# Output weights loaded during the projection's last phase, activation rows loaded far ahead, and another load table for phase 2's weights, in a hybrid decoder layer

## The chip, the cores and the metric

The kernel runs on one core of a Trainium2 chip. The metric is the time of one execution on the device in microseconds (us). The engines go by the profile's names: PE (matmul; PEld is its weight load), DVE (vector), ACT (scalar), POOL (GpSimd) and SP, which here only issues DMAs. Each engine takes its instructions in the order of its own list.

## The reference

One layer of a decoder is computed for 4096 prompt tokens and 64 sample tokens. All is fp32.

```python
h = rmsnorm(x, g_pre)                     # x: 4096 (and 64) x 1024
z = h @ w_in                              # 1024 x 2816, cut into ten column groups
out_a = silu(cg) * cb * conv3(cc * ch)    # gated short convolution
out_b = silu(ag) * window_attention(q, k, v, sinks)   # window of 128, 8 heads, 2 kv heads
out_c = silu(mg) * cross_attention(mq, mem_k, mem_v)  # 4 heads, 256 memory tokens
y = concat([out_a, out_b, out_c]) @ w_out # 1024 x 1024
x = x + rmsnorm(y, g_post)
```

Memory keys and values come from another normalised product (`w_mem_kv`). The last rows of the window's keys and values and of the convolution's input are outputs as well.

## The kernel before, in words

**Precision.** A matmul operand is split in two parts: hi, a cast to fp32r on ACT, and lo, the rest, a subtract on DVE. A product is three matmuls: hi by hi, lo by hi, hi by lo. `w_split` (L144) does so for a weight tile of 128x512: `S.copy` (L145) and `V.tensor_tensor` (L146).

**Input projection.** The 4160 tokens are 8 blocks of 520. The 22 column groups of 128 of `w_in` are taken as 11 pairs in three phases: phase 1 (index 0) has 4 pairs, phase 2 (index 1) 4 and phase 3 (index 2) 3. Within a phase each block is computed by seven block products in the manner of Strassen and Winograd (`PRODUCTS`): the weights A11, A12, A22 come from `w_in`, S1 to S4 are sums of them; the activations are B11 to B22 and their sums T1 to T4. In each step of a block one product is done for each pair (L305), and its result is added to z (`evict`, L312 on DVE, L314 on ACT). A step (phase, block, product) is the unit of all tables. The first two blocks of phase 1 are "plain": eight steps (block, step) each, since the sums of weights are made beside them. `plain_jobs` (L554) lists what ACT, DVE and POOL do after each plain step, `plain_loads` (L584) what SP loads. In phases 1 and 2 the order of each engine's list is that of the program. In phase 3 and in attention a scheduler sets it.

**Row statistics.** Each token needs 1/rms of its row. The rows (104 at a time) are loaded by `row_load` (L208) into `nat` tiles of a pool with two buffers; `row_step` squares and sums one (ACT L227), asks for the load two further on, and after five of them POOL computes r (L231, L232) and stores it to DRAM as `rowd` (L236). `row_queue` (L253) issues the waiting nat loads and the loads of `rb` (L206), r spread over all partitions. For the first blocks r goes to the token axis through a diagonal (`rows_diag`, DVE L243) and a product (`rows_product`, PE L249, ACT L251). After that, x is scaled ahead of the split (L271, L275) instead of z behind the product; this is the type change.

**Weights.** Split weights lie in two pools of slots of 4 KB per partition: `wa` (21 slots, pairs 0 to 2) and `wb` (7 slots, pair 3). Raw weights are loaded (`w_load` L152) into `temp` tiles, which the gates `th` (L365, L366), their stores to `md` and z's halves use too. The table `SWITCH` (L752) says in which steps phase 2's weights are loaded (`next_loads`, into `temp` tiles, or with `True` into the two nat buffers) and split (`next_fills`); `last` is block 7. POOL issues the stores of th to `md` until phase 2 begins, SP from then on.

**Attention.** `open_attention` (L828) closes the projection's pools and opens `fix` (constants, and `wo`, the split output weights), `mixp` (three buffers of `mix`, 1 MB each, L920), and `wor` (three raw buffers). 16 chunks of 256 tokens go through window units (L998 to L1031) and cross units (L958 to L973) of a pipe. In the first two chunks, each of 16 starts of the pipe also issues one load of half a row group of `w_out` (`wo_load`, L1047) and the split of the one before (`wo_split`, L1052 on ACT, L1053 on DVE). After them come the blocks of the output projection: `mix` is split to `mh` and `ml` (L1252, L1253), multiplied by `wo` (L1270), normalised and stored, with the units of later chunks in between.

Of the kernel before, what the change touches and what calls it, by code (L numbers as in the profile page):

```python
# [51 lines left out]
def hybrid_layer(ctx: ExitStack, tc: tile.TileContext, a: dict):  # L52
# [31 lines left out]

    pa = ExitStack()
    wa = pa.enter_context(tc.tile_pool(name="wa", bufs=3 * NP_))
# [57 lines left out]
    def w_split(w, raw):  # L144
        S.copy(w[:, 0], raw)  # L145
        V.tensor_tensor(w[:, 1], raw, f(w[:, 0]), op=ALU.subtract)  # L146
# [53 lines left out]
    nat, sq = {}, [0]  # L200
# [7 lines left out]
    def row_load(j):  # L208
        if j < 5 * NBLK:
            g = RG * j - NS  # L210
            t = nat[j] = natp.tile([P, D], F32, tag="nat", name=f"nat{j}")
            if g < 0:
                DMA.dma_start(t[:NS], a["x_s"])
                DMA.dma_start(t[NS:RG], a["x_p"][: RG - NS, :])
            else:
                DMA.dma_start(t[:RG], a["x_p"][g : g + RG, :])

    def row_step():
# [9 lines left out]
        row_loads.append(j + 2)  # L228
# [251 lines left out]
    def next_block(ph, b, p):  # L480
# [11 lines left out]
        if ph == 0:  # L492
            jobs.append(row_queue)
            if 1 <= p < 6 or (b, p) == (PLAIN_BLOCKS, 0):
                jobs.append(row_step)
# [58 lines left out]
    def plain_jobs(b, s):  # L554
# [29 lines left out]
    def plain_loads(b, s):  # L584
        for o in {(0, 0): ["A22"], (0, 1): ["A12"]}.get((b, s), ()):
            first_w(o)
        if (b, s) == (0, 0):
            row_load(0)
            row_load(1)
        for nb, o in {(0, 1): [(0, "B12")], (0, 2): [(0, "B22")], (0, 3): [(1, "B11")], (0, 4): [(1, "B21")],  # L590
                      (0, 6): [(1, "B12")], (0, 7): [(1, "B22")], (1, 1): [(2, "B11")], (1, 2): [(2, "B21")],
                      (1, 4): [(2, "B12")], (1, 5): [(2, "B22")]}.get((b, s), ()):
            x_of(0, nb, o)
        row_queue()
# [48 lines left out]
    def third_start():  # L643
        keep = right.enter_context(tc.tile_pool(name="memkv", bufs=1, side="right"))
        third["mk"] = keep.tile([P, 2, 4, 256], F32R, name="mk")
        third["mkv"] = keep.tile([P, 2, 512], F32, name="mkv")
        third["pre"] = pre_stack.enter_context(tc.tile_pool(name="pre", bufs=1, side="right"))
# [116 lines left out]
    def input_projection():  # L764
        for i, (ph, b, p) in enumerate(steps):
# [62 lines left out]
    def open_attention():  # L828

        nonlocal ps, fix, mixp, qp, pp, wor  # L830
# [5 lines left out]
        fix = ctx.enter_context(tc.tile_pool(name="fix", bufs=1))  # L836
        mixp = ctx.enter_context(tc.tile_pool(name="mixp", bufs=3))
        qp = att.enter_context(tc.tile_pool(name="qp", bufs=2))
        pp = att.enter_context(tc.tile_pool(name="pp", bufs=2))
        wor = pre_stack.enter_context(tc.tile_pool(name="wor", bufs=3, side="right"))  # L840

    ps = fix = mixp = qp = pp = wor = None
# [43 lines left out]
    class Chunk:  # L886
# [30 lines left out]
        def load_mix(self):  # L917

            self.mix = mixp.tile([P, KT, CT], F32, tag="mix", name=f"mix{self.c}")
# [69 lines left out]
        def window_unit(self, i, kvh, steps):  # L989
# [3 lines left out]
            for half in range(2):  # L993
# [7 lines left out]
                V.copy_predicated(sm[:, 2 * half : 2 * half + 2, :], wmask, negs if first else s3[:, :, 0:P])  # L1001
# [3 lines left out]
            V.scalar_tensor_tensor(nm, mx, -SCALE, nsink[:, 4 * kvh : 4 * kvh + 4], op0=ALU.mult, op1=ALU.min)  # L1005
            es = tiny.tile([P, 4], F32, tag="es", name=f"wes{b}_{kvh}")
            V.tensor_tensor(es, nm, sink[:, 4 * kvh : 4 * kvh + 4], op=ALU.add)
# [34 lines left out]

    wo_raw = {}

    def wo_load(i):
        wo_raw[i] = wor.tile([P, 512], F32, tag="wr", name=f"wor{i}")
        DMA.dma_start(wo_raw[i], a["w_out"][i // 2][:, 512 * (i % 2) : 512 * (i % 2) + 512])  # L1047

    def wo_split(i):
        cs = slice(512 * (i % 2), 512 * (i % 2) + 512)  # L1050
        w, raw = wo[i // 2], wo_raw.pop(i)
        S.copy(w[:, 0, cs], raw)  # L1052
        V.tensor_tensor(w[:, 1, cs], raw, f(w[:, 0, cs]), op=ALU.subtract)  # L1053
# [139 lines left out]
    sink = fix.tile([P, 8], F32, name="sink")  # L1193
    nsink = fix.tile([P, 8], F32, name="nsink")
    wmask = fix.tile([P, 2, P], U8, name="wmask")
    negs = fix.tile([P, 2, P], F32, name="negs")
    gpost = fix.tile([P, D], F32, name="gpost")
    wo = [fix.tile([P, 2, D], F32R, name=f"wo{k}") for k in range(KT)]
    DMA.dma_start(sink, a["sinks"].partition_broadcast(P))
# [247 lines left out]
```

## Time and profile before

| | |
|---|---|
| median of 3 runs | 1678.74 us (1677.52 to 1679.97) |
| the profiled execution's own time | 1678.51 us |
| its span in the profile | 1676.8 us |
| PE busy | 1585.2 us (95%) |
| DVE, ACT, POOL busy | 1184.1, 791.1, 352.5 us |
| HBM read, written | 196.81 MB, 108.12 MB |
| mean granted clock of PE | 0.975 |

Stages by the trace: phase 1 up to about 380 us, phase 2 up to about 713, phase 3 up to 973.6, attention and the output projection from there to the end. The page's groups give busy time, the mean of one instruction, and the idle time before it with what ended it. A row of waits reads: engine and line, what it waited for, us in total, times, longest. A chain of waits lists start, length and instruction or transfer, each released by the one above it. A granted clock of 1.00 is full speed.

### The profile page before, as it was taken

The page shows a single profiled execution, that of the slowest core. Times are in us where ns is not written, and L with a number is a line of the kernel's source. Part 1 is how long each engine was busy: PE and PEld are TensorE (multiplying, and loading weights), DVE is VectorE, ACT ScalarE, POOL GpSimd, SP SyncE. Part 2 cuts the span into 40 slices and gives each one's busy share as a digit, 9 for nine tenths or more (in the row PEclk, how much of TensorE's full clock was granted, in tenths as well). Part 3 has the DMA queues.
Part 4 walks back from the last instruction along what each step waited for, and adds up shares of the span by engine and source line. Part 5 has one row for each costly group of instructions (what it writes and reads, how often), then busy time and mean ns, then how long its engine had stood idle before and what let it go on. Part 6 is the DMA issues. An engine that isn't in the chain of part 4 may idle for free.

```text
span 1676.8 us, 29593 instructions
## 1 busy us (share of the span) xinstructions
PE 1585.2 (95%) x11077; PEld 1401.8 (84%) x11077; DVE 1184.1 (71%) x2124; ACT 791.1 (47%) x2023; POOL 352.5 (21%) x590
## 2 busy tenths in 40 slices
PE   7967999998999999999999956999999999999998
PEld 7967999998999999998999944677777777777766
DVE  5657878898888778974666656766767667767743
ACT  5665656565222222543333336555555555555522
POOL 0213222211000000000000025444333443343320
PEclk9989999999999999999999977999999999999999
DMA  8777999868755333689667497767777666666152
GB/s 228 142 232 183 264 269 261 235 231 284 194 188 177 117 116 127 217 244 283 223 214 255 157 252 146 131 143 143 152 158 157 151 136 135 148 149 132 51 185 88
DMA packets 175235, 305.89 MB, mean 182 GB/s; under 512 B 31093, under 2 KB 104565, under 8 KB 175061
## 3 DMA queue, kind: packets, MB, share of 16 engines
q1 hardware_dynamic: 128917, 228.08, 44.2%
q0 software_dynamic: 46176, 75.92, 22.9%
q8 instruction: 88, 1.44, 0.4%
q14 instruction: 54, 0.44, 0.1%
HBM read 196.81 MB, written 108.12 MB: 182 GB/s over the span
## 4 chain that ended last, share of the span: by engine, by line
PE 55%; DVE 18%; DMA 9%; ACT 8%; issue 5%; POOL 4%; SPq 0%; ACTq 0%; POOLq 0%; DVEq 0%
PE c L305 42%; PE y L1270 6%; ACT sm L1011 5%; DMA nat<-in_x_p 3%; DVE sm L1017 3%; DVE sm L1001 2%; DMA wor<-in_w_out 2%; DVE wmx L1003 2%; POOL xp L966 2%; DVE yn L1277 1%; PE wt L1021 1%; DMA rowd<-r 1%; PE xs L958 1%; DMA md<-th 1%; DVE mix L985 1%
## 5 line engine op out<-in xcount | busy, mean ns | idle before, releaser
L1270 PE MATMUL y<-wo,mh 128*128 128x512 f32 (+1 forms) x1072 | 351.9, 392 | 1.4 <-DVE mh L1247 1.4
L312 DVE TENSOR_TENSOR z<-c,z 128x520 f32<-128x520 f32 (+1 forms) x308 | 194.7, 646 | 98.1 <-PE c L305 94.8
L1270 PEld LDWEIGHTS y<-wo,mh 128*128 128x128 f32 x1072 | 201.1, 189 | 42.1 <-issue 2.8
L1270 PE MATMUL y<-wo,ml 128*128 128x512 f32 (+1 forms) x520 | 202.7, 390 | 0.0
L1011 ACT ACTIVATE sm<-sm,wnm 128x128 f32<-128x128 f32 x256 | 99.8, 391 | 75.8 <-DVE wnm L1005 75.8
L1270 PEld LDWEIGHTS y<-wo,ml 128*128 128x128 f32 x520 | 98.5, 190 | 15.4
L998 PE MATMUL ws<-kst,q 128*128 128x256 f32 x512 | 81.2, 300 | 7.8 <-ACT sm L1000 5.7
L1028 POOL TENSOR_SCALAR_AFFINE_SELECT wpv<-wpt 128x512 f32<-128x512 f32 x62 | 40.2, 648 | 224.8 <-ACT wpt L1023 224.0
L998 PEld LDWEIGHTS ws<-kst,q 128*128 128x128 f32 x512 | 67.9, 196 | 10.2 <-ACT sm L1000 6.2
L959 DVE TENSOR_REDUCE xmx<-xs 128x2 f32<-128x512 f32 x64 | 44.2, 691 | 43.4 <-PE xs L958 43.4
L900 POOL MEMSET kst<- 128x512 f32 x1 | 0.5, 531 | 345.1 <-DMA wr_2A<-in_w_in 345.1
L962 ACT ACTIVATE xp<-xs,xnm 128x256 f32<-128x256 f32 x128 | 59.4, 470 | 27.1 <-DVE xnm L960 26.8
L966 POOL TENSOR_SCALAR xp<-xp,xrd 128x256 f32<-128x256 f32 x128 | 63.4, 503 | 38.2 <-DVE xrd L963 35.4
L1000 ACT COPY sm<-ws 128x256 f32<-128x256 f32 x128 | 44.6, 371 | 56.4 <-PE ws L998 53.5
L1278 ACT ACTIVATE y<-y 128x512 f32<-128x512 f32 (+1 forms) x66 | 38.8, 588 | 66.5 <-DVE yn L1277 66.5
L1277 DVE TENSOR_TENSOR yn<-y,gpost 128x512 f32<-128x512 f32 (+1 forms) x66 | 45.1, 684 | 31.9 <-PE y L1270 31.8
L1288 DVE SCALAR_TENSOR_TENSOR xr<-yn,yst,xr 128x1024 f32<-128x1024 f32 (+2 forms) x34 | 42.5, 1253 | 30.3 <-POOL yst L1284 30.3
L1021 PEld LDWEIGHTS wt<-ident,sm 128*128 128x128 f32 x256 | 28.3, 145 | 40.7 <-issue 18.2
L958 PE MATMUL xs<-mk,q 128*128 128x256 f32 x256 | 48.4, 313 | 13.4 <-ACT xp L962 8.5
L227 ACT ACTIVATE nat<-nat 104x1024 f32<-104x1024 f32 x40 | 42.3, 1058 | 38.2 <-DMA nat<-in_x_p 38.2
L1017 DVE TENSOR_TENSOR sm<-sm,wrd 128x512 f32<-128x512 f32 x64 | 55.0, 860 | 2.1
L1021 PE MATMUL wt<-ident,sm 128*128 128x128 f32 x256 | 42.8, 292 | 14.0 <-DVE sm L1017 8.1
(956 smaller groups left out, 5108.5 us busy)
## 6 DMA issues: line engine op xcount, KB each, us to landing
q<-qd POOLq DMA_DIRECT2D x64, 384.0 KB, 5.0
mix<-md SPq DMA_DIRECT2D x16, 1024.0 KB
xr<-in_x_p SPq DMA_DIRECT2D x32, 512.0 KB
nat<-in_x_p SPq DMA_DIRECT2D x39, 416.0 KB
o_yp<-xr SPq DMA_DIRECT2D x31, 512.0 KB
md<-th POOLq DMA_DIRECT2D x48, 260.0 KB, 7.3
qd<-zh SPq DMA_DIRECT2D x48, 260.0 KB
qd<-z SPq DMA_DIRECT2D x48, 260.0 KB
```

The lines of the kernel that those rows point to most:

```text
L305: TE.matmul(bank[:, :HW], l, r, start=first and i == 0, stop=last and i == 3 * KH - 1)
L312: add = lambda dst, other: V.tensor_tensor(dst, c, other, op=ALU.add)
L958: TE.matmul(s[:, i, :], q[:, i * P : i * P + P], third["mk"][:, part, h, :], start=part == 0, stop=part == 1)
L962: S.activation(p[:, i, :], s[:, i, :], AF.Exp, bias=nm[:, i : i + 1], scale=SCALE, accum_out=den[:, i : i + 1])
L966: G.tensor_scalar(p[:, i, :], p[:, i, :], rd[:, i : i + 1], 0.5, op0=ALU.mult, op1=ALU.mult)
L998: TE.matmul(s3[:, hh, :], self.q[:, 4 + 2 * (2 * half + hh) + kvh, i * P : i * P + P], self.kst[:, 2 * kvh + part, i * P : i * P + 2 * P], ...
L1000: S.copy(sm[:, 2 * half : 2 * half + 2, :], s3[:, :, P : 2 * P])
L1011: S.activation(sm[:, hh, :], sm[:, hh, :], AF.Exp, bias=nm[:, hh : hh + 1], scale=SCALE, accum_out=den[:, hh : hh + 1])
L1017: V.tensor_tensor(sm, sm, rd.unsqueeze(2).to_broadcast([P, 4, P]), op=ALU.mult)
L1021: TE.transpose(t[:, hh * P : (hh + 1) * P], sm[:, hh, :], ident)
L1270: TE.matmul(acc, self.hl[l][:, k], wo[k][:, r, c0:c1], start=j == 0, stop=j == passes * KT - 1)
L1277: V.tensor_tensor(yn[:m, c0:c1], acc[:m], gpost[:m, c0:c1], op=ALU.mult)
```

## The change

1. *Output weights.* `wa` stays open to the end. In the last block of phase 3, steps 1 to 6, three (at last one) of 16 half tiles of `w_out` are loaded per step into `temp` tiles and split in the next step into `wa` slots, as these become free of phase 3's weights. The casts of `w_split` keep the program's order on ACT from phase 2 on. The 16 loads and splits among the pipe's starts are gone, and so are the pools `fix` and `wor`. `mh`, `ml` and `gpost` take `wa` slots; `mixp` has two buffers, and every third `mix` lies in `yp`, which opens earlier. The sinks and the mask are loaded at the start of phase 3.
2. *Rows.* nat tiles 2 to 9, 12 and 13 lie in `wa` and `wb` slots that are idle then, and are loaded in steps (0,1) to (0,7); the later ones follow on through the two buffers. The loads of nat 2 and 3 and of B12's activations are now ahead of A12's weights on SP. The row squares stand earlier in `plain_jobs`, the diagonal after step (1,3) instead of (1,4); one sum of weights' fill (pair 3, S1) moves from (0,7) to (1,4).
3. *Phase 2's weights.* Another `SWITCH` table: A11 and A12 and S2 are loaded and split earlier in the last block of phase 1, S3 and S1 are split one step later in phase 2's first block.

```diff
+    wa = ctx.enter_context(tc.tile_pool(name="wa", bufs=3 * NP_))
     pa = ExitStack()
-    wa = pa.enter_context(tc.tile_pool(name="wa", bufs=3 * NP_))
...
     def w_split(w, raw):
-        S.copy(w[:, 0], raw)
+        copy = S.copy(w[:, 0], raw)
+        if store_queue[0] is DMA:
+            tc.keep_in_program_order(copy)
...
-            t = nat[j] = natp.tile([P, D], F32, tag="nat", name=f"nat{j}")
+            if 2 <= j < 10 or 12 <= j < 14:
+                t = (wa if j < 7 or j == 12 else wb).tile([P, 2, 512], F32, tag="w", name=f"nat{j}")
+                t = nat[j] = t.rearrange("p a n -> p (a n)")
+            else:
+                t = nat[j] = natp.tile([P, D], F32, tag="nat", name=f"nat{j}")
...
-        row_loads.append(j + 2)
+        if j in (10, 11) or j >= 14:
+            row_loads.append(after_nat[0])
+            after_nat[0] += 1
...
-            (0, 5): lambda: [*sums(1, 0), *sums(1, 1), *fills(1, "S2", "S3"), *row],
-            (0, 6): lambda: [*parts(1, "B11"), *fills(1, "S1", "S4"), *row, *sums(3, 0), *row],
-            (0, 7): lambda: [*fills(3, "S2", "S3", "S1"), *row],
+            (0, 5): lambda: [*sums(1, 0), *row, *sums(1, 1), *fills(1, "S2", "S3"), *row],
+            (0, 6): lambda: [*parts(1, "B11"), *row, *fills(1, "S1", "S4"), *sums(3, 0), *row],
+            (0, 7): lambda: [*row, *fills(3, "S2", "S3")],
             (1, 0): lambda: [*parts(1, "B21"), *z_rows(0, 1), *row, *row],
-            (1, 1): lambda: [*z_rows(0, 0), *done(0, 1), *row],
-            (1, 2): lambda: [*parts(1, "B12"), *row, *done(0, 0), *row],
-            (1, 3): lambda: [*row, *sums(2, 0), *sums(2, 1), *fills(2, "S2")],
-            (1, 4): lambda: [*parts(1, "B22"), lambda: rows_diag(), *gains(2, "B11", "B21"), lambda: rows_product()],
-            (1, 5): lambda: [*row, *fills(2, "S3", "S1", "S4"), *scales(2, "B11")],
-            (1, 6): lambda: [*gains(2, "B12"), *scales(2, "B21", "B12"), *row, *row],
+            (1, 1): lambda: [*z_rows(0, 0), *done(0, 1), *row, *row],
+            (1, 2): lambda: [*parts(1, "B12"), *done(0, 0), *row],
+            (1, 3): lambda: [*sums(2, 0), *sums(2, 1), *fills(2, "S2"), lambda: rows_diag(), *row],
+            (1, 4): lambda: [*parts(1, "B22"), *fills(3, "S1"), *gains(2, "B11", "B21"), lambda: rows_product(), *row],
+            (1, 5): lambda: [*fills(2, "S3", "S1", "S4"), *scales(2, "B11"), *row],
+            (1, 6): lambda: [*gains(2, "B12"), *scales(2, "B21", "B12"), *row],
...
+        for j in {(0, 0): (0, 1), (0, 1): (2, 3), (0, 2): (4, 5, 6), (0, 3): (7, 8, 9), (0, 4): (10,), (0, 5): (11,),
+                  (0, 7): (12, 13)}.get((b, s), ()):
+            row_load(j)
...
-    SWITCH = {(0, last, 1): lambda: next_loads("A11", True),
-              (0, last, 2): lambda: next_loads("A12"),
-              (0, last, 3): lambda: next_fills("A11"),
-              (0, last, 4): lambda: [*next_fills("A12"), *next_loads("S2", True)],
-              (0, last, 6): lambda: next_fills("S2"),
+    SWITCH = {(0, last - 1, 6): lambda: next_loads("A11", True),
+              (0, last, 1): lambda: [*next_fills("A11"), *next_loads("A12"), *next_loads("S2", True)],
+              (0, last, 3): lambda: [*next_fills("A12"), *next_fills("S2")],
               (1, 0, 0): lambda: next_loads("S3"),
-              (1, 0, 1): lambda: [*next_loads("S1"), *next_fills("S3")],
-              (1, 0, 2): lambda: [*next_loads("S4"), *next_fills("S1")],
-              (1, 0, 3): lambda: next_loads("A22"),
+              (1, 0, 1): lambda: next_loads("S1"),
+              (1, 0, 2): lambda: [*next_fills("S3"), *next_loads("S4")],
+              (1, 0, 3): lambda: [*next_fills("S1"), *next_loads("A22")],
...
+    def wo_load(j):
+        k, h = divmod(j, 2)
+        wo_raw[j] = temp(f"wor{j}")[:, :512]
+        DMA.dma_start(wo_raw[j], a["w_out"][k][:, 512 * h : 512 * h + 512])
+
+    def wo_split(j):
+        k, h = divmod(j, 2)
+        wo[k][h] = wa.tile([P, 2, 512], F32R, tag="w", name=f"wo{k}_{h}")
+        w_split(wo[k][h], wo_raw.pop(j))
...
+            if ph == 2 and b == last and p > 0:
+                for j in range(3 * p - 3, min(3 * p, 2 * KT)):
+                    jobs.append(lambda j=j: wo_load(j))
+                    pending.setdefault(i + 1, []).append(lambda j=j: wo_split(j))
...
-            wo_load(i)
-            if i > 0:
-                wo_split(i - 1)
             if i == 9:
+                pre_stack.close()
+                yp = ctx.enter_context(tc.tile_pool(name="yp", bufs=2, side="right"))
                 chunk_load(2)
...
+            parts = lambda n: wa.tile([P, 2, 512], F32R, tag="w", name=n).rearrange("p a (b n) -> p (a b) n", n=P)
-            hi = yp.tile([P, KT, P], F32R, tag="mh", name=f"mh{b}")
+            hi = parts(f"mh{b}")
...
-            lo = yp.tile([P, KT, P], F32R, tag="ml", name=f"ml{b}")
+            lo = parts(f"ml{b}")
```

More of the change, by code (lines that the diff above doesn't have):

```diff
@@ L199, in hybrid_layer @@
     rows = {}
-    nat, sq = {}, [0]
+    nat, sq, after_nat = {}, [0], [14]
     row_loads, row_spreads = [], {}
@@ L593, in plain_loads @@
             x_of(0, nb, o)
+        if (b, s) == (0, 1):
+            first_w("A12")
         row_queue()
@@ L646, in third_start @@
         third["mkv"] = keep.tile([P, 2, 512], F32, name="mkv")
+        sink, nsink = (keep.tile([P, 8], F32, name=n) for n in ("sink", "nsink"))
+        third["sink"], third["nsink"] = sink, nsink
+        wmask = third["wmask"] = keep.tile([P, 2, P], U8, name="wmask")
+        negs = third["negs"] = keep.tile([P, 2, P], F32, name="negs")
+        tc.keep_in_program_order(DMA.dma_start(sink, a["sinks"].partition_broadcast(P)))
+        V.tensor_scalar(nsink, sink, -1.0, None, op0=ALU.mult)
+        tc.keep_in_program_order(DMA.dma_start(negs, a["wmask"]))
+        G.tensor_copy(wmask, negs)
+        G.memset(negs, NEG)
         third["pre"] = pre_stack.enter_context(tc.tile_pool(name="pre", bufs=1, side="right"))
@@ L828, in open_attention @@
     def open_attention():
-        nonlocal ps, fix, mixp, qp, pp, wor
+        nonlocal ps, mixp, qp, pp
         own.close()
@@ L917, in load_mix @@
         def load_mix(self):
-            self.mix = mixp.tile([P, KT, CT], F32, tag="mix", name=f"mix{self.c}")
+            self.mix = (yp if self.c % 3 == 2 else mixp).tile([P, KT, CT], F32, tag="mix", name=f"mix{self.c}", bufs=1 if self.c % 3 == 2 else 2)
             DMA.dma_start(self.mix, md[:, :, self.ts].rearrange("k p n -> p k n"))
@@ L1040, in chunk_load @@
             chunks[c].load_queries()
[L1043 to L1053, printed above, removed]
     def transpose_to(dst, srcs, name):
@@ L1192, in hybrid_layer @@
     open_attention()
[L1193 to L1199, printed above, removed]
-    wmf = wor.tile([P, 2, P], F32, tag="wr", name="wmf")
-    DMA.dma_start(wmf, a["wmask"])
-    G.tensor_copy(wmask, wmf)
-    V.tensor_scalar(nsink, sink, -1.0, None, op0=ALU.mult)
-    G.memset(negs, NEG)
     chunk_load(1)
@@ L1222, in hybrid_layer @@
                 chunks[2].load_mix()
-    wo_split(15)
+    gpost = wa.tile([P, 2, 512], F32, tag="w", name="gpost").rearrange("p a n -> p (a n)")
     DMA.dma_start(gpost, a["gpost"].partition_broadcast(P))
     G.tensor_scalar(gpost, gpost, float(D) ** 0.5, None, op0=ALU.mult)
-    pre_stack.close()
-    yp = ctx.enter_context(tc.tile_pool(name="yp", bufs=2, side="right"))
     class Block:
```

24 lines of the change are left out of this document (10 added, 14 removed).

## The prediction

> **What bounds the kernel now.** I read the page first, for what fills the span, then a table by stage, then the waits of TensorE (PE) stage by stage, and the chain of waits behind each large one. The page:
>
> ```profile
> span 1676.8 us, 29593 instructions
> PE 1585.2 (95%) x11077; PEld 1401.8 (84%) x11077; DVE 1184.1 (71%) x2124; ACT 791.1 (47%) x2023; POOL 352.5 (21%) x590
> ```
>
> PE is busy for 1585.2 of 1676.8 us, so 91.6 us are all that better cover could return directly, plus whatever it loses at a low clock. The change takes no product away: only stages where PE stands count. The table by stage, with PE's busy time second, the granted clock behind POOL's column, and the share and rate of DMA last:
>
> ```profile
> core 0: us, PE busy (x) PEld busy (x) DVE busy (x) ACT busy (x) POOL busy (x), PEclk, DMA share, GB/s
> 1.20:28.50 27.30, 19.41 (x141) 19.19 (x142) 12.62 (x23) 13.92 (x26) 0.34 (x2) 1.00 0.97 282
> 86.00:100.00 14.00, 0.87 (x6) 0.70 (x5) 9.27 (x19) 7.25 (x17) 2.47 (x4) 0.63 0.99 298
> 100.00:118.00 18.00, 18.00 (x135) 17.62 (x135) 5.70 (x7) 10.92 (x22) 1.69 (x3) 0.91 0.45 148
> 118.00:147.00 29.00, 20.40 (x161) 19.28 (x159) 19.50 (x22) 15.30 (x28) 9.88 (x13) 0.95 0.73 175
> 147.00:165.00 18.00, 18.00 (x135) 18.00 (x136) 14.48 (x19) 10.62 (x21) 1.68 (x3) 0.89 0.72 207
> 380.00:402.00 22.00, 14.94 (x100) 14.53 (x100) 15.96 (x20) 11.02 (x19) 3.78 (x7) 0.84 0.96 349
> 402.00:436.00 34.00, 34.00 (x286) 34.00 (x286) 33.55 (x55) 16.45 (x29) 0.00 (x0) 1.00 0.61 165
> 943.80:973.60 29.80, 29.78 (x248) 29.57 (x246) 18.46 (x26) 10.49 (x15) 0.00 (x0) 1.00 0.32 120
> 973.60:1043.60 70.00, 37.78 (x166) 24.67 (x168) 38.92 (x104) 35.42 (x125) 27.70 (x41) 0.68 0.95 205
> 1043.60:1657.00 613.40, 605.32 (x3304) 448.97 (x3301) 413.54 (x1006) 323.88 (x1193) 229.78 (x389) 0.99 0.63 140
> ```
>
> Four places lose time that the change touches: the rows' sums at 86 to 100, the type change at 118 to 147, the change to phase 2's weights at 380 to 402, and above all the start of attention, where PE is busy for 37.78 of 70 us at a clock of 0.68. From 1043.6 on PE is busy for 605.32 of 613.40: that part moves as one block, and the change adds no instruction to it.
>
> **The change part by part.**
>
> *Rows loaded far ahead.* What ended PE's wait, then the chain of waits up to it (start, length, what):
>
> ```profile
> PE rows_y L249 <- DVE diag L243: 13.1, 1, 13.1
> ```
>
> ```profile
> 71.98 9.69 DMA rowd<-r
> 81.68 0.34 SPq L206
> ...
> 82.54 11.42 DMA nat<-in_x_p
> ...
> 98.92 0.65 DVE diag L243 x3
> ```
>
> SP issues its DMAs in order. Its load of rb (L206) waits 9.69 us for the store of rowd, and the next nat loads stand behind it; they also need one of two buffers. ACT's squares, the diagonal on DVE and PE's row product follow. With rows 2 to 9, 12 and 13 in idle weight slots, these loads pass neither rb nor the two buffers, the 15th square stands in step (1,2)'s jobs instead of (1,3)'s, and the diagonal is ahead of step (1,4)'s other jobs. The chain needs some 13 us less for PE to find the diagonal ready; it loses a wait of 9.69 and a load of 11.42, 21 together. So I take all 13.1. PE's clock of 0.91 over the next 18 us costs 0.09 x 18 = 1.6; I take 1 of it. **Rows: -14** (bounds -5, if half the squares still come late, to -15).
>
> What is late next? The loads moved ahead of A12's weights. The first cast of those weights, and PE's first three products, from the timeline and the chain of waits:
>
> ```profile
> 22.64 0.62 ACT L145 CAST w_0A<-wr_0A 128x512 fp32r<-128x512 f32 x1 [4.07 <-DMA wr_0A<-in_w_in]
> ```
>
> ```profile
> 9.09 20.02 PE c L305 x144
> ```
>
> ```profile
> nat<-in_x_p SPq DMA_DIRECT2D x8, 416.0 KB
> xl0B<-in_xt SPq DMA_DIRECT2D x2, 520.0 KB
> ```
>
> Two nat loads and one x load, 2 x 416 + 520 = 1352 KB, now go first; at the 282 GB/s of 1.2 to 28.5 that is 4.9 us, so this cast starts at 27.5, ends at 28.1, and its DVE subtract (0.7) at 28.8. PE's fourth product starts at 9.09 + 20.02 = 29.1. It fits by 0.3 us: cost 0 taken, +3 at worst (with the clock that it would drop). By the Trainium skill ("DMA: Bandwidth & Descriptors", section "Queues, rings and completion order"), each DMA engine takes the descriptors of one ring in ring order, and SP owns one ring on each; by that rule the whole 4.9 us falls on A12. The 4.07 us that ACT waits even now, for a load that SP issues behind the two nat loads, agree with it.
>
> *The type change.* The chain of waits and PE's wait:
>
> ```profile
> 128.66 2.30 POOL r L231
> ...
> 131.04 1.19 POOL r L232
> ...
> 132.52 0.50 POOL rowd L236
> ...
> 133.52 8.44 DMA md<-th
> 141.99 0.63 ACT zh L346
> ```
>
> ```profile
> PE c L305 <- ACT hi_2T L295: 6.9, 2, 6.5
> ```
>
> POOL computes r and issues rowd before it issues the stores of th; zh on ACT needs the buffer that the first of these stores frees, and hi_2T (PE's operand) stands behind zh. In the changed order the square that feeds this r comes before the casts of th, three ACT places earlier, so r and rowd (2.30 + 1.19 + 0.50 on POOL) are done when th is. The first store then goes out near 125 instead of 133.5 and lands before zh wants it. The 6.5 us go, and about 1 of the 2.0 us (0.11 x 18) of low clock behind them. DVE is next: it has 19.5 us of work in 29, so I take **-7** (bounds 0 and -9).
>
> *The weights of phase 2.* PE's waits, and the chain ahead of the second one:
>
> ```profile
> PE c L305 <- ACT z L314: 4.4, 1, 4.4
> PE c L305 <- DVE lo_0B L296: 2.7, 1, 2.7
> PE c L305 <- ACT hi_1T L295: 1.7, 1, 1.7
> ```
>
> ```profile
> 385.83 7.13 DMA wr_3S<-sd6S
> ...
> 393.50 0.59 ACT z L314
> ```
>
> A split, a cast on ACT and a subtract on DVE of 128x512, has its price in the groups of the tile wo (least, median and most ns, then first and last start):
>
> ```profile
> L1052 ACT CAST wo<-wor x16: 612/618/642, 974.0 to 1038.7; 128x512 fp32r<-128x512 f32 x16
> L1053 DVE TENSOR_TENSOR wo<-wor,wo x16: 672/684/1154, 975.1 to 1042.4; 128x512 fp32r<-128x512 f32 x16
> ```
>
> ACT reaches the cast of w_3S before its load has landed, and the eviction of z, which frees PE's accumulator, stands behind it. A step of this phase is 48 matmuls, 48 x 34/286 = 5.7 us by the row of 402 to 436. The new table puts S3's casts one step later, nearly the 7.13 that the load takes. S2's four casts and subtracts move from step 6 of the last block to step 3, so lo_0B is not behind them: 4 x 0.68 = 2.7 us. That removes 4.4 + 2.7 = 7.1, and the clock of 0.84 costs 0.16 x 14.94 = 2.4, of which I take 1.5. Against it: step 3 gets eight splits, 5.4 us of DVE in a 5.7-us step, and at 402 to 436 DVE has 33.55 us of work in 34, so splits pushed there can return as a longer wait at hi_1T. **-8** (bounds +2 and -11).
>
> *The output weights.* What ACT waits for at the start of attention, and the longest pieces of the chain:
>
> ```profile
> ACT wo L1052 <- DMA wor<-in_w_out: 19.5, 7, 7.9
> ```
>
> ```profile
> 980.62 13.47 DMA wor<-in_w_out
> ...
> 995.48 12.16 DMA wor<-in_w_out
> ...
> 1023.88 8.89 DMA wor<-in_w_out
> ```
>
> Three raw buffers, refilled by SP behind one-megabyte mix loads, take 12 to 13 us a turn, and ACT, in order, makes the softmax wait for them. Out of this stage go the 19.5 us of waits and the 16 casts of 0.62 (all start from 974.0 on; 9.9): 29.4. A part returns, because the softmax's own waits for PE and DVE lay beside some of these. From the other side: the stage moved 70 x 205 = 14.4 MB; without 16 x 256 KB = 4.2 MB, 10.2 MB remain, 50 us at the same rate, a saving of 20. I take 20 (bounds -10, if most of the waits return, and -30, with the clock). By the Trainium skill ("DMA: Bandwidth & Descriptors", "Specifications"), one core's HBM limit is about 358 GB/s; by that figure the 10.2 MB would need 28 us and DMA would bound nothing here; the 205 measured is the nearer guide, since the stage's share is 0.95 already.
>
> Where they go: the last block of phase 3 from 943.8 to 973.6, where DMA is at 0.32, DVE at 18.46 and ACT at 10.49 of 29.8 us. 16 subtracts (10.9) make DVE 29.4, 16 casts (9.9) make ACT 20.4. It fits, with DVE full: a step (29.8/7 = 4.3 us) has 1.6 us of DVE idle for three subtracts of 2.05. The last stores come later by the rest: 0.43 x 6 = 2.6 us, of which I take 1 as the loss, the splits of the last load lying behind PE's last step. So **-20 + 1 = -19** (bounds -8 and -30). The buffers of mix, mh and ml keep their number, so nothing is added later; the scale of gpost and the sinks' loads are off PE's path on both sides.
>
> The change from phase 2 to 3, whose largest wait of PE is
>
> ```profile
> PE c L305 <- DVE lo_0B L296: 1.7, 1, 1.7
> ```
>
> keeps its tables and its lists of loads: 0.
>
> Sum: -14 - 7 - 8 - 19 = -48. The profiled execution took 1678.5 us (span 1676.8, and 1.7 around it), 0.2 below the median of the three runs: **1678.5 - 48 = 1630**.
>
> **The rivals.**
> - *The last block of phase 3 waits for the output weights* (the slower end). Three loads a step need raw buffers that the stores of z use too, and ACT's casts, pinned in program order, stand ahead of hi of the next step. If a turn takes as long there as at 980 (13.47 us) instead of a step's 4.3, each of six turns adds 9.2: +55, and 1630 + 55 = 1685. It decides the sign from turns of 12.4 us on (48.5/6 + 4.3). Against it: DMA's share is 0.32 there, against 0.95 where the 13.47 was measured. Chance 0.06.
> - *The start of attention is bound by its own latencies:* only the casts' 9.9 us are gained there instead of 20: 1640. For it: wt, xs and ws of PE wait for DVE and ACT in turn even where no wo stands between. Chance 0.15.
> - *DVE takes the bound at both type and weight changes:* neither 7 nor 8 is gained: 1645. For it: 33.55 of 34. Chance 0.15.
> - *The rows do not come in time*, because another in-order wait (rb behind rowd, A12 late) holds ACT: 14 not gained, 3 lost at A12: 1647. This is the change not doing what it says. Chance 0.12.
> - *Several of these at once:* about 1660 to 1680. Chance 0.07.
>
> **How the numbers follow.** The forecast of 1630, within about 15, holds 0.45. The rivals up to 1647 hold 0.42. The range takes the forecast's better end (all waits and clocks: about 1614) and reaches to the lower half of the combined case: 1614 to 1662, about 0.8. A measurement can tell about 0.2% (3.4 us) from no change: faster by more 0.91, the same 0.03, slower 0.06.
>
> **What would show it.** PE's wait at rows_y gone and no wait of ACT for nat between 40 and 100; no wait of PE over 2 us for hi_2T; no wait of PE for the eviction z at the start of phase 2; the first cast of mh about 20 us closer to the end of phase 3, which itself ends about 28 us earlier; and the steady part again about 613 us. I would be wrong if PE waits in the last block of phase 3, if w_0A of A12 is cast after 29, or if the time from the end of phase 3 to the first mh stays near 70 us.

## The result, and the profile after

The changed kernel takes 1654.75 us (median of 4 runs, 1653.01 to 1656.55) against 1678.32 for the kernel before (median of 4): ratio 0.9858, 95% interval 0.9841 to 0.9876. That is 23.6 us less, where 48 were forecast. The profiled execution took 1654.18 us. Its page:

```profile
span 1652.3 us, 29582 instructions
PE 1578.8 (96%) x11077; PEld 1398.6 (85%) x11077; DVE 1181.4 (71%) x2124; ACT 789.3 (48%) x2023; POOL 346.9 (21%) x590
```

The work is the same, so the difference lies in PE's waits and clock. To see where, I divided both spans at instructions of PE that have the same place in both: the row product, a product of block 4 and one of phase 2's first block, one of phase 3's first block, the first transpose of the values, and the last block of the output projection. From the timeline of PE, before:

```profile
99.70 2.07 PE L249 MATMUL rows_y<-diag,ones 104*128 104x260 f32 x4 [13.13 <-DVE diag L243]
247.29 0.39 PE L305 MATMUL c<-lo_4T,w_0A 128*128 128x260 f32 x1 [0.56 <-DVE lo_4T L296]
440.18 0.39 PE L305 MATMUL c<-lo_1T,w_0S 128*128 128x260 f32 x1 [0.21 <-DVE lo_1T L296]
719.84 0.39 PE L305 MATMUL c<-lo_0B,w_0A 128*128 128x260 f32 x1 [1.69 <-DVE lo_0B L296]
974.66 0.33 PE L927 MATMUL vtp<-ident,vT 128*128 128x128 f32 x1 [1.08 <-DVE z L312]
1651.86 0.50 PE L1270 MATMUL y<-wo,mh 128*128 128x512 f32 x1 [1.43 <-DVE mh L1247]
```

And after:

```profile
97.83 0.77 PE L258 MATMUL rows_y<-diag,ones 104*128 104x260 f32 x1 [9.98 <-DVE diag L252]
237.92 0.39 PE L314 MATMUL c<-lo_4T,w_0A 128*128 128x260 f32 x1 [1.69 <-DVE lo_4T L305]
430.42 0.59 PE L314 MATMUL c<-lo_1T,w_0S 128*128 128x260 f32 x1 [1.42 <-DVE lo_1T L305]
712.53 0.59 PE L314 MATMUL c<-lo_0B,w_0A 128*128 128x260 f32 x1 [4.55 <-DVE lo_0B L305]
967.86 0.33 PE L961 MATMUL vtp<-ident,vT 128*128 128x128 f32 x1 [0.91 <-DVE z L321]
1627.41 0.73 PE L1277 MATMUL y<-wo,mh 128*128 128x512 f32 x2 [1.38 <-DVE mh L1254]
```

The differences of the starts give the terms of the forecast one by one:

| stretch | before | after | change | forecast |
|---|---|---|---|---|
| start to the row product | 99.70 | 97.83 | -1.9 | rows: -14 |
| to block 4 | 147.59 | 140.09 | -7.5 | type change: -7 |
| to block 1 of phase 2 | 192.89 | 192.50 | -0.4 | phase 2's weights: -8 |
| to block 0 of phase 3 | 279.66 | 282.11 | +2.5 | 0 |
| to the values' transpose | 254.82 | 255.33 | +0.5 | output weights: +1 |
| to the last output block | 677.20 | 659.55 | -17.7 | output weights: -20 |
| rest | 24.94 | 24.89 | 0 | 0 |

Two terms are right (type change, output weights); two are missing, 12 us at the rows and 8 at phase 2's weights, and 2.5 are lost at a place that was forecast unchanged. The table by stage, in the columns of the earlier one:

```profile
86.00:98.00 12.00, 2.02 (x17) 1.84 (x16) 6.07 (x14) 3.31 (x8) 2.66 (x5) 0.76 0.62 188
425.00:440.00 15.00, 10.38 (x69) 10.05 (x70) 12.05 (x19) 3.67 (x5) 0.00 (x0) 0.77 0.81 187
937.40:967.00 29.60, 29.55 (x246) 29.35 (x244) 24.01 (x37) 16.14 (x25) 0.00 (x0) 1.00 0.72 239
967.00:1018.00 51.00, 29.68 (x152) 20.52 (x152) 30.89 (x90) 29.97 (x114) 18.91 (x33) 0.80 1.09 233
1018.00:1632.00 614.00, 606.17 (x3313) 449.89 (x3314) 414.11 (x1008) 324.27 (x1195) 234.04 (x395) 0.99 0.62 139
```

The hole at 86 to 98 is still there, a larger one than before lies at 425 to 440 (PE busy for 10.38 of 15 us), the last block of phase 3 takes the splits beside PE's work (29.55 of 29.60), and the start of attention shrank from 70 to 51 us.

**The rows.** The chain of waits that ends at the diagonal in the changed kernel:

```profile
48.43 11.85 DMA rowd<-r
60.30 6.04 DMA rb<-rowd
66.36 4.70 DVE z L560 x4
...
71.97 9.28 DMA md<-th
...
81.34 0.65 ACT th L374
...
83.23 1.16 ACT nat L234 x2
...
84.76 1.16 POOL r L241
85.92 5.86 DMA md<-th
91.79 0.69 DVE wa2A L538
...
97.13 0.56 DVE diag L252 x3
```

The last square now starts at 83.23, not at 94.04, so the rows do come in time. But DVE's diagonal stands behind the sums of pair 2's weights (wa2A) in step (1,3), and these need temp tiles that the stores of th (md) give back. That second chain starts with the first five rows' r, goes over rowd, rb, z and th, and was almost as long before the change: z was scaled at 68.2 then, at 66.36 now. It took over. The last square hangs on it as well: it stands behind th (81.34) in ACT's list, and th waits for a store of th (md) that lands just ahead.

**Phase 2's and phase 3's start.** What PE waits for at the two places, in the changed kernel (the three largest of seven waits, then the largest of two):

```profile
PE c L314 <- ACT hi_1T L304: 3.7, 1, 3.7
PE c L314 <- ACT z L323: 1.5, 1, 1.5
PE c L314 <- DVE lo_1T L305: 1.4, 1, 1.4
```

```profile
PE c L314 <- DVE lo_0B L305: 4.6, 1, 4.6
```

The waits that the table was to remove did shrink (z from 4.4 to 1.5, lo_0B in block 0 from 2.7 to 0.3), but hi_1T and lo_1T one block later grew from 1.9 to 5.1 together.

**The end of phase 3.** ACT's timeline there, after:

```profile
967.65 1.24 ACT L145 CAST wo<-wor 128x512 fp32r<-128x512 f32 x2 [2.48 <-DMA wor<-in_w_out]
969.03 1.24 ACT L355 CAST zh<-z 128x520 fp32r<-128x520 f32 x2
...
972.97 0.62 ACT L145 CAST wo<-wor 128x512 fp32r<-128x512 f32 x1 [1.93 <-DMA wor<-in_w_out]
973.72 0.62 ACT L355 CAST zh<-z 128x520 fp32r<-128x520 f32 x1
979.01 0.43 ACT L963 COPY vt<-vtp 128x128 f32<-128x128 f32 x2 [4.66 <-DMA qd<-z]
```

The last casts of z stand behind casts that wait for output weights. From the values' first transpose to the copy vt it now takes 11.2 us (967.86 to 979.01), before 5.3 (974.66 to 979.93): some 6 us of the gain of attention are given back here, and the whole of attention still gains 17.7, so 23.5 behind vt.

### The profile page after: what moved, and what is told of

Its sections match the earlier page's. It is cut to its first block, busy times and chain, and to the rows that moved or that the text cites. A ratio compares the mean times of both kernels' runs of the same rounds, so it can differ in the third digit from the quotient of the medians.

```text
span 1652.3 us, 29582 instructions
## 1 busy us (share of the span) xinstructions
PE 1578.8 (96%) x11077; PEld 1398.6 (85%) x11077; DVE 1181.4 (71%) x2124; ACT 789.3 (48%) x2023; POOL 346.9 (21%) x590
## 3 DMA queue, kind: packets, MB, share of 16 engines
q0 software_dynamic: 46176, 75.92, 23.5%
## 4 chain that ended last, share of the span: by engine, by line
PE 55%; DVE 18%; DMA 8%; issue 8%; ACT 7%; POOL 4%; SPq 0%; ACTq 0%; DVEq 0%; POOLq 0%
PE c L314 37%; PE y L1277 9%; ACT sm L1045 4%; DMA md<-th 2%; DVE sm L1051 2%; DVE sm L1035 2%; DVE wmx L1037 2%; PE wt L1055 2%; PE wo L918 1%; POOL xp L1000 1%; PE xs L992 1%; PE ws L1032 1%; DVE yn L1284 1%; DMA nat<-in_x_p 1%; DVE xr L1295 1%
## 5 line engine op out<-in xcount | busy, mean ns | idle before, releaser
L937 POOL DMA_DIRECT2D kst<-qd x64 | 38.9, 624 | 254.4 <-DMA qd<-z 188.1
L1032 PE MATMUL ws<-kst,q 128*128 128x256 f32 x512 | 80.0, 298 | 12.1 <-ACT sm L1034 11.4
L1032 PEld LDWEIGHTS ws<-kst,q 128*128 128x128 f32 x512 | 67.1, 195 | 14.6 <-ACT sm L1034 11.9
L1005 PEld LDWEIGHTS xt<-ident,xp 128*128 128x128 f32 x256 | 29.3, 140 | 31.3 <-PE wo L918 12.2
```

The lines of the kernel that those rows point to most:

```text
L1032: TE.matmul(s3[:, hh, :], self.q[:, 4 + 2 * (2 * half + hh) + kvh, i * P : i * P + P], self.kst[:, 2 * kvh + part, i * P : i * P + 2 * P], ...
```

## The experiments

All are compared with the kernel before on the same chip, which took 1677.8, 1679.1, 1679.0 and 1676.6 us (medians) beside the four groups of runs. Intervals are of the ratio to it. Executions of one program differ by up to 15 us (the kernel before, in one group: 1667.8 to 1683.3). So only larger differences are read from the times, and a wait from one profile counts for more where other profiles repeat it. Times of different groups are compared by their ratios.

**1 to 3: each part alone**, the kernel before with the rows' part, with the table `SWITCH`, or with the output weights' part, each exactly as in the diff of the change.

> The kernel before with the rows' part alone (far-ahead row loads, new plain tables). Theory A (read from the trace after the change): the squares come earlier, but the diagonal on DVE now stands behind the sums of weights, which wait for a temp tile held by a store of th; PE's wait at rows_y stays at 8 to 11 us, the A12 weights come 1 us late, and only the type change gains its 7: about 1669 to 1671. Theory B (the forecast's own terms): -14 and -7, about 1657.

Measured: 1668.83 us, ratio 0.9947 (0.9929 to 0.9966), PE's wait at rows_y (the row product) 9.6. As theory A has it, but for A12's weights: their first cast starts at 27.48, and PE does not wait for it.

> The kernel before with the new load table for phase 2's weights alone. Forecast: -8, about 1670. Theory A (the gain is given back within 50 us, because the loads of x for the next block now stand behind the loads of S and A22 weights on SP, and DVE has no idle time): -2 to +1, about 1676 to 1679, with a wait of PE for hi_1T of over 3 us.

Measured: 1675.26 us, 0.9988 (0.9971 to 1.0006). In its profile PE's waits at that place add to 5.5 us (z 3.0, lo_1T 1.7, hi_1T 0.5, lo_0B 0.3) against 8.9 before: the table is worth 3.4, between the two theories, and no wait for hi_1T grows. So theory A's reason, the loads of x behind the loads of weights on SP, falls.

> The kernel before with the output weights' part alone, which also pins the casts of all weight splits from phase 2 on. Forecast: -19, about 1659. Theory A (the start of attention gains over 20, but the last stores of phase 3 come about 6 us later behind the casts that wait for output weights, and the pinned casts cost about 3 at the change from phase 2 to 3): about -15, 1663.

Measured: 1665.95 us, 0.9927 (0.9900 to 0.9954). Its profile has the loss at phase 3 with the old table and the old row loads:

```profile
PE c L308 <- DVE lo_0B L299: 4.7, 1, 4.7
```

So that loss belongs to the output weights' part. Its time falls short of the forecast and of theory A, but its profiled execution was the fastest of four (1660.27): in it attention takes 658.5 us instead of 677.2, and the stretch to phase 3 283.0 instead of 279.7. The parts alone give -8.9, -2.5 and -11.8, together -23.3: they add up to the whole change, and each is worth less than forecast by itself.

**4: the diagonal first.**

```diff
-        t = nat["diag"] = temp("diag")[:RG, : 2 * HW]
+        t = nat["diag"] = wb.tile([P, 2, 512], F32, tag="w", name="diag").rearrange("p a n -> p (a n)")[:RG, : 2 * HW]
...
-            (1, 3): lambda: [*sums(2, 0), *sums(2, 1), *fills(2, "S2"), lambda: rows_diag(), *row],
-            (1, 4): lambda: [*parts(1, "B22"), *fills(3, "S1"), *gains(2, "B11", "B21"), lambda: rows_product(), *row],
+            (1, 3): lambda: [lambda: rows_diag(), *sums(2, 0), *sums(2, 1), *fills(2, "S2"), *row],
+            (1, 4): lambda: [*parts(1, "B22"), *gains(2, "B11", "B21"), lambda: rows_product(), *fills(3, "S1"), *row],
```

> The changed kernel with the diagonal ahead of the sums of weights in step (1,3), in a weight slot instead of a temp tile, and the split of pair 3's S1 behind the row product. Theory A (the diagonal was late only through DVE's order and the temp tile): PE's wait at rows_y falls from 10 us to under 2 and the time by 7 to 9, to about 1646. Rival (r itself is late, or PE then waits for the S2 weights instead): the wait stays or moves to a product, and the time stays within 3 us of 1654.7.

Measured: 1655.12 us, 0.9865 (0.9839 to 0.9891). The wait at rows_y is gone, but the product behind it waits as long for ACT's copy rb_first (L260), which frees PE's accumulator; ACT in turn stands at the cast of w_2S, behind the same sums:

```profile
PE c L314 <- ACT rb_first L260: 9.6, 1, 9.6
```

```profile
ACT w_2S L145 <- DVE wa2A L545: 9.6, 1, 9.6
```

The rival's sentence is met and theory A's mechanism too: the sums hold whatever is queued behind them, on either engine.

**5: one more temp tile.** The split of S1 goes back to (0,7) in `plain_jobs`, and nat 13 to the two buffers.

> The changed kernel with the split of pair 3's S1 back in step (0,7), and nat 13 through the two nat buffers again to make room for it. Theory A (of seven temp tiles one is held by S1's sum from step (0,6) to (1,4), so DVE's sums of pair 2 and the gates th run out of tiles): DVE's wait at wa2A for a store of th falls from 6.3 us to under 2 and PE's wait at rows_y from 10 to under 6, the time by 4 to 9. Rival (the stores of th are late whatever the number of tiles, or the load of nat 13 now holds ACT): PE's wait stays at 8 to 12 us.

Measured: 1653.65 us, 0.9846 (0.9822 to 0.9870), PE's wait 7.1 instead of 10.0; DVE's wait for md moved by one tile, from wa2A to wa2S, and stayed at 6.8. Half of theory A: one tile more moves the wait, it does not end it.

**6: r on POOL behind the stores of th.**

```diff
-            (1, 2): lambda: [*parts(1, "B12"), *done(0, 0), *row],
-            (1, 3): lambda: [*sums(2, 0), ...
+            (1, 2): lambda: [*parts(1, "B12"), *done(0, 0)],
+            (1, 3): lambda: [*row, *sums(2, 0), ...
```

> The changed kernel with the 15th row's square, and with it r on POOL, in step (1,3) behind the issue of the second three stores of th, instead of in step (1,2) ahead of it. Theory A (POOL, in order, waits for that square before it issues these stores): the first of them is issued about 3 us earlier, near 82.7 instead of 85.9, DVE's wait at wa2A falls by about 3 us, and so does PE's at rows_y (10 to about 7). Rival (the landing of the stores, bound by a full DMA, decides): no change.

Measured: 1650.05 us, 0.9823 (0.9800 to 0.9847). The store is issued at 82.63 as expected, and DVE's wait at wa2A is 0.5; PE's wait is still 8.4:

```profile
82.63 7.54 DMA md<-th
90.19 0.70 DVE wa2A L538
```

The sums start 1.6 us sooner (90.19, not 91.79). POOL's order held the store for 3 us, of which the landing took half back. The time is 4.7 under the changed kernel's, more than the 1.6 of this wait, but the two intervals just overlap.

**7: only the output weights' casts pinned.**

```diff
     def w_split(w, raw, pin=False):
         copy = S.copy(w[:, 0], raw)
-        if store_queue[0] is DMA:
+        if pin:
             tc.keep_in_program_order(copy)
...
-        w_split(wo[k][h], wo_raw.pop(j))
+        w_split(wo[k][h], wo_raw.pop(j), True)
```

> The changed kernel in which only the output weights' casts are pinned in program order, not all casts of weight splits from phase 2 on. Theory A (the pinned casts draw nine subtracts on DVE ahead of the work that ends the block, so that lo_0B is late): PE's wait for lo_0B at the start of phase 3 falls from 4.6 us to about 1.7, as before, and the time by about 3. Rival (the sinks' loads and nsink on DVE at that place do it): the wait stays over 4 us.

Measured: 1645.42 us, 0.9807 (0.9779 to 0.9835), some 9 under the changed kernel. PE's waits at phase 2's start and at phase 3's:

```profile
PE c L313 <- ACT z L322: 3.3, 1, 3.3
PE c L313 <- DVE lo_1T L304: 1.7, 1, 1.7
PE c L313 <- ACT hi_1T L303: 0.5, 1, 0.5
PE c L313 <- DVE lo_0B L304: 0.3, 1, 0.3
```

```profile
PE c L313 <- DVE lo_0B L304: 2.0, 1, 2.0
PE c L313 <- ACT hi_0B L303: 1.3, 1, 1.3
```

The pinned casts were the cost at both places. At phase 3 lo_0B falls from 4.6 to 2.0; at phase 2 all waits of PE from 8.1 (seven) to 5.9 (four), near the 5.5 that the table alone has. The other runs repeat it. All eight profiles with the pins wait 4.5 to 4.7 us for lo_0B, all nine without them 1.7 to 2.0. With the new table, PE waits 3.6 to 3.7 for hi_1T in all seven profiles with the pins and 0.5 to 0.9 in all six without; a part of this comes back at z (1.4 to 1.6 with the pins, 3.0 to 5.1 without). By the stretches of the first section, block 4 to block 1 of phase 2 takes 186.9 us instead of 192.5, and from there to phase 3's block 278.6 instead of 282.1; some 3 us of the first difference are the granted clock (1.00 against 0.96 from 360 to 440 us) and not waits. At 0.96, runs 2, 10, 13 and 14, without the pins, still take 187.1 to 188.3 us for the first stretch, and the seven profiles with the pins and the new table 189.8 to 192.5.

**8: output weights one step earlier** (loads in steps 0 to 5 of the last block).

> The changed kernel with the loads of the output weights, and so their splits, one step earlier in the last block of phase 3 (from step 0 on). Theory A (the last casts wait for output weights ahead of the last casts of z, so the last stores of phase 3 and with them the values' transposes come late): from the end of the last product to the first cast of vt it takes about 6 us instead of 12, and the time falls by 4 to 6. Rival (four temp tiles for gates, stores and output weights are the limit, wherever the loads begin): PE waits in that block and nothing is gained.

Measured: 1655.32 us, 0.9848 (0.9817 to 0.9880). From the transpose to vt 8.7 us (973.49 to 982.19) instead of 11.2, and attention from there to the last output block takes 656.4 instead of 659.6; but the stretch before it, from phase 3's first block, grew from 255.3 to 257.7, of which 1.3 are waits of PE that the profile lists (lo_7B, lo_7T, and z ahead of the transpose). Theory A's mechanism is there, and nothing is gained, as the rival has it.

**9: the sums behind the row product.** As run 4, with both sums and the S2 split of pair 2 moved:

```diff
+            (1, 3): lambda: [lambda: rows_diag(), *row],
+            (1, 4): lambda: [*parts(1, "B22"), *gains(2, "B11", "B21"), lambda: rows_product(),
+                             *sums(2, 0), *sums(2, 1), *fills(2, "S2"), *fills(3, "S1"), *row],
```

> The changed kernel with the diagonal in a weight slot as in the fourth run, and the sums and the S2 split of pair 2 moved behind the row product, into step (1,4). Theory A (what held the diagonal, and in the fourth run ACT's copy of rb_first, are only the temp tiles that those sums wait for): neither rows_y nor the product behind it waits over 2 us near 90 to 105, and the time falls by 7 to 9 from the changed kernel's, to about 1646. Rival (something else, a load of x or the next hi, is as late): a wait of 5 us or more stays there.

Measured: 1646.46 us, 0.9812 (0.9778 to 0.9847), 8 under the changed kernel, and at rows_y

```profile
PE rows_y L258 <- DVE diag L252: 0.6, 1, 0.6
```

Theory A. The row product starts at 84.79 instead of 97.83, a gain of 13.0, of which the type change takes some back: block 4 comes at 231.2, 6.7 us sooner than in the changed kernel. Even with the diagonal in time, only half of the wait comes back.

**10: the last four output weights behind the last stores**, with the edit of run 7.

> The seventh run's kernel (only the output weights' casts pinned) with the last four half tiles of w_out loaded and split behind the last stores of phase 3. Theory A (the last z casts stand behind casts that wait for those loads): the last product to the first cast of vt falls from 12 us to 7 or 8, the time by 3 to 5 from that run's 1645. Rival (the wait moves into the first softmax, since ACT then waits for the four loads there): same time within 2 us.

Measured: 1649.83 us, 0.9827 (0.9792 to 0.9862), with executions from 1643.0 to 1653.0. From the transpose to vt it takes 8.3 us instead of 10.7 in run 7, so theory A's wait does shrink. But the last cast of output weights then waits for its load, and the first softmax (sm) stands behind it, 12.2 us after the transpose instead of 11.0:

```profile
962.72 3.23 DMA wor<-in_w_out
965.97 0.63 ACT wo L145
...
967.39 0.38 ACT sm L1037
```

The rival, as to the place. Attention from the transpose to the last output block takes 661.2 us instead of 657.9 in run 7. The time cannot tell by how much: the two intervals overlap.

**11: run 7 with the table of before.**

> The seventh run's kernel with the table of before for phase 2's weights. Theory A (without the pinned casts the new table is worth about 3 us, as in the second run): about 3 us slower than the seventh run, near 1648. Rival (the table is worth its forecast 8 once nothing is pinned): near 1653. Rival 2 (nothing): 1645.

Measured: 1652.35 us, 0.9847 (0.9816 to 0.9878), near the first rival, but its interval overlaps with run 7's. PE's waits at phase 2's start add to 6.4, against 5.9 in run 7; the granted clock from 360 to 440 us is 0.94 against 1.00. Of the 6.9 us between these two kernels the waits show 0.5; what makes up the rest stays open.

**12: all three edits** (runs 7, 9 and 10 together).

> The changed kernel with the three edits together: only the output weights' casts pinned, the sums of pair 2 behind the row product, the last four output weights behind the last stores. If the three places are independent, the gains add: -7 to -9, -8, and -3 to -5 from 1654.7: about 1634 to 1637. If a later wait takes one of them back: 1640 or more.

Measured: 1643.57 us, 0.9790 (0.9762 to 0.9819): less than the sum. Besides run 10's loss, the profiled execution waits 6.7 us at rows_y. Its chain:

```profile
49.26 13.22 DMA rowd<-r
62.49 10.17 DMA rb<-rowd
72.69 4.70 DVE z L559 x4
...
78.30 7.91 DMA md<-th
...
87.98 1.16 ACT nat L233 x2
...
90.92 0.46 DVE diag L251 x2
```

In run 9 rowd and rb took 12.18 and 5.13 us, and z started at 64.18. With the sums out of the way, the same chain still reaches the diagonal over ACT: the last square stands behind th, which waits for a store of th. How late that is depends on the landings of rowd, rb and md.

**13: runs 7 and 9 together.**

> The twelfth run's kernel without the late output weights: only the output weights' casts pinned, the sums of pair 2 behind the row product. Theory A (the late output weights gave in attention what they won at the end of phase 3): attention, from the values' first transpose to the last block, takes 658 us again instead of 661, and the time is 2 to 4 under the twelfth run's, near 1640. Rival (no difference): 1643 to 1645.

Measured: 1639.72 us, 0.9781 (0.9761 to 0.9800), PE's wait at rows_y 0.5. Attention takes 658.9 us against 661.5 in run 12, as theory A has it; the time is not clear of run 12's, whose interval overlaps. It is the fastest kernel here, 13 us under the changed one by the ratios (15 by the medians), with run 14 level.

**14 and 15: the row loads spread**, in run 13's kernel and in the changed one.

```diff
-        for j in {(0, 0): (0, 1), (0, 1): (2, 3), (0, 2): (4, 5, 6), (0, 3): (7, 8, 9), (0, 4): (10,), (0, 5): (11,),
-                  (0, 7): (12, 13)}.get((b, s), ()):
+        for j in {(0, 0): (0, 1), (0, 1): (2, 3), (0, 2): (4,), (0, 3): (5, 6), (0, 4): (7, 10), (0, 5): (8, 11),
+                  (0, 6): (9,), (0, 7): (12, 13)}.get((b, s), ()):
```

> The thirteenth run's kernel with the far-ahead row loads spread over steps (0,2) to (0,6), one or two a step instead of three. Theory A (the rows loaded three a step fill DMA just when the B22 half of block 0 and the store and load of the first r are wanted, and the chain from that r over z and th to the row product starts late): hi of B22 is cast at 38 instead of 41, the first rowd lands sooner than 12 us after its issue, PE's wait at rows_y, where one is left, shrinks, and the time falls by 2 to 5. Rival (that store is slow at any load): no change within 2 us.

Measured: 1639.99 us, 0.9785 (0.9762 to 0.9808): no change. Theory A misses: hi of B22 is cast at 40.5, rowd still took 11.47 us to land, and PE waits 4.5 at rows_y, since a store of th took 12.48 us and held th and the square behind it on ACT. Yet block 4 starts at 230.9, against 231.6 in run 13: a row product 4.6 us later cost nothing there.

> The changed kernel with the row loads spread in the same way and nothing else. Theory A: the whole chain that ends at the diagonal comes 2 to 4 us sooner, so PE's wait at rows_y falls from 10 us to 6 to 8. Rival: it stays at 9 to 12.

Measured: 1656.66 us, 0.9887 (0.9861 to 0.9913), PE's wait 9.4: the rival. How many rows are loaded a step does not decide this wait.

## Why the prediction was right in part, and where it failed

- *Rows, -14 forecast, -1.9 measured.* The step that failed is "So I take all 13.1". The nat chain did get shorter (the last square starts at 83.23, not 94.04; ACT still waits 4.3 us for nat between 40 and 100, 18.2 before). But the second chain to the same instruction was put at nothing: the diagonal's place on DVE, behind sums that wait for tiles held by th's stores. With the sums out of the way, PE's wait of 10.0 falls to 0.6 (run 9) and 0.5 (run 13); run 4 shows that they hold ACT too. They are not all of it: in runs 12 and 14, without them, the same chain still costs 6.7 and 4.5 over ACT's square. And the term was too large even for a diagonal in time, since of 13.0 us at the row product 6.7 reach block 4 (run 9). The forecast gave the place a rival ("another in-order wait (rb behind rowd, A12 late) holds ACT", 0.12, 14 not gained and 3 lost). The 14 were nearly all missed, but the engine that held the diagonal was DVE, and A12 cost 1.3.
- *A12's weights, 0 forecast, PE waits 1.06 and 0.22 us for them.* The first cast started at 28.95 and not at 27.5. The estimate of 4.9 us was 1.4 short here. In the 14 profiles with these loads ahead the cast starts at 27.48 to 29.44, and PE waits 0 to 2.0: the margin of 0.3 was smaller than what executions differ by. The rule of the Trainium skill ("DMA: Bandwidth & Descriptors", section "Queues, rings and completion order") agrees in kind: the whole delay of 6.3 us (22.64 to 28.95) fell on the load that was put behind the others.
- *Type change, -7 forecast, -7.5 measured.* The wait of 6.5 for hi_2T is gone, as worked out: the first store of th goes out at 124.5 (near 125 was forecast), and zh follows th without a wait. The stretch takes 138.5 to 144.2 us in the nine profiles with this order, 147.5 to 149.3 in the three with the order before, so the agreement to half a microsecond is luck, the size is not.
- *Phase 2's weights, -8 forecast, -0.4 measured.* Two steps failed. "That removes 4.4 + 2.7 = 7.1" took z's wait of 4.4 from one profile. The 2.7 of lo_0B do go (0.3), but z still waits 3.0 with the table alone (run 2), and in the other profiles with the old table (runs 1, 3 and 11) z waits only 1.7 to 1.8. So the table takes away 3.4 us of waits against the kernel before, and under 1 against runs 1 and 11. The other step is the 0 for the change from phase 2 to 3 ("keeps its tables and its lists of loads"). The pinned casts of w_split, which the forecast met only in a rival and for the last block of phase 3, put 2.2 us of waits back at phase 2's start and 2.6 at phase 3's first lo_0B (run 7): the +2.5 where 0 was forecast.
- *Output weights, -19 forecast, -17.2 measured* (-17.7 and +0.5). The step is right. Inside it, the cost of the last casts was taken at 1 and is 6 between the products' end and vt, and the gain behind that was taken at 20 and is 23.5, so the near sum is in part luck. So is the stage's length (51 us, 50 worked out): it moved 11.9 MB at 233 GB/s, where 10.2 MB at 205 were assumed. That DMA bounds it is not shown by that. By the HBM limit of the Trainium skill ("DMA: Bandwidth & Descriptors", "Specifications") these 11.9 MB would have needed about 33 us, an estimate from 358 GB/s, so that figure was no bound here.
- *The slower rival did not come:* the loads cost PE nothing in the last block (29.55 of 29.60 busy). DVE is busy there for 24.01 us and not for the 29.4 worked out, and three of the 16 splits come behind the block. The rival's turn of 13.47 us was the longest of the three shown, the shortest 8.89.

What stays open: which of landing time and clock makes executions of one of these programs differ by up to 15 us, and why the first 2-KB store of rowd takes 11.4 to 13.2 us in the changed kernels (9.35 before) even with the row loads spread. How the pinned casts make hi_1T late at phase 2's start is not shown either. At phase 3 the trace agrees with run 7's theory A, but for the count: between the lo_0B before and the late one DVE takes six subtracts of weights (starts 698.71 to 705.44) in the changed kernel and three in run 7.

## What to carry to other kernels

When a stall goes, look for the second chain into the same instruction, on its own engine's list: everything queued ahead of it there, with the tiles that each waits for, has to be priced as if the first chain were gone. A line that fixes an order is part of the change in every place where its function is called, and worth a run by itself. Moving work into an idle stage pays (17 us here), but its last pieces cost some us wherever they stood: ahead of the stage's own last stores, a step earlier (run 8), or just ahead of the next stage's first step (run 10). A wait that a forecast is to remove is worth reading in more than one profile.

## What the runs showed of the hardware

A store of 2 KB issued by POOL (rowd) took 8.7 to 12.5 us to land in the kernel before (seven stores, median 10.1) and 8.9 to 14.3 in the changed one (median 12.0): its size says nothing of its landing. The first of them took 8.8 to 9.5 in the three profiles with the old row loads and 11.4 to 13.2 in nine with the new ones (the changed kernel and runs 1, 4, 7, 8, 9, 11, 12 and 14). DMA's share while it was in flight was no higher after (0.52 from 48 to 60.5 us) than before (0.60 from 46 to 56); in the stretch ahead of it, from 28.5 to 45 us, it was 0.94 after and 0.54 before. That the busier stretch is the cause is not shown. Five profiled kernels with the same order of work up to there (the changed one and runs 7, 8, 10, 11) waited 8.7 to 12.1 us at the same row product.
